# Fifteen of the eighteen adaLN vectors as running sums on the vector engine, in a two-layer hybrid DiT

## The chip, the cores and the metric

One core of a Trainium2 chip runs the whole program in one launch. The metric is the time on the device in microseconds; the number compared is the median of several runs. Engines: PE is the tensor engine (PEld its weight loads), DVE the vector engine, ACT the scalar engine, POOL GpSimd, SP the engine whose queue issues most DMAs.

## The reference: what is computed

Two layers over an image stream (512 tokens, x) and a context stream (256 tokens, c), each of 1024 features, all in float32. Each layer is a half FFN (hidden size 2816), a token mixing of three kinds (gated linear attention, sliding-window attention, RWKV7) with in- and out-projections, and a second half FFN. Nine vectors of 1024 per layer and stream, made from a conditioning vector, shift, scale and gate the three sub-layers:

```python
def adaln_params(cvec, w, b):
    m = jax.nn.silu(cvec) @ w + b              # [D] @ [D, 9 D]
    return m.reshape(cvec.shape[0], 1, N_MOD, D_MODEL)

def modulate(h, m, i):
    return h * (1.0 + m[:, :, 3 * i + 1]) + m[:, :, 3 * i]

def half_ffn(h, m, i, wg, wu, wd, g, b):
    u = modulate(h, m, i)
    return post_norm(h, 0.5 * m[:, :, 3 * i + 2] * swiglu(u, wg, wu, wd), g, b)

for l in range(DEPTH):                         # DEPTH = 2
    m_x = adaln_params(c, w_ada[l], b_ada[l])
    m_c = adaln_params(c_ctx[None], w_ada[l], b_ada[l])
    h_x = half_ffn(h_x, m_x, 0, ...)           # and h_c
    mix_x, mix_c = token_mixing(modulate(h_x, m_x, 1), modulate(h_c, m_c, 1), ...)
    h_x = post_norm(h_x, m_x[:, :, 5] * (mix_x @ w_out[l]), ...)
    h_x = half_ffn(h_x, m_x, 2, ...)           # h_c too, but not in the last layer
```

The 18 vectors (9 per layer, "vector 0" to "vector 8") take two products of a vector of 1024 with a matrix of 1024 x 9216 per layer. In layer 1 the context needs vectors 0 to 4 alone.

## The kernel before

Features lie on the partitions: a stream is 8 k-tiles of [128, tokens]. Every large product takes its operands as hi + lo parts, three PE products per pair (`product`); a block of weights, 4 k-tiles of 128 columns, is loaded by SP (`r_...`), copied by ACT to the hi part (`h_...`) and subtracted to the lo part (`l_...`) by DVE and POOL in turn (`load_split`). An FFN (`ffn`) makes 22 hidden tiles in six groups, two products each (`pg`, `pu`), and after each group eight down products (`py`), which DVE adds to the residue `r`. Names carry the stream, the layer and the FFN: `pgc00_4` is the gate product of hidden tile 4 of the context, layer 0, FFN 0.

The order of the program is `first(C)`, `mix(C, 0)`, `first(X)`, `mix(X, 0)`, `rest(C, 0)`, `mix(C, 1)`, `rest(X, 0)`, `mix(X, 1)`, `rest(X, 1)`, but a list scheduler with a model of the engines sets the order on each engine when the program is built, so that parts run beside each other: the context's mixing runs inside the image's FFN, and the image's mixing inside the context's later FFNs. On the chip each engine's queue runs in that order.

adaLN is cut into 72 chunks, 36 per layer, of 256 columns, four to a vector. A chunk (`ada_chunk`) is four loads of 256 KB (`wa`, eight buffers, later three) and eight PE products with 32 columns of the conditioning vectors (`sc`) as stationary and 256 columns of weights as moving operand. Four k-tiles go to four groups of 32 rows of a bank. After a vector's fourth chunk DVE copies the bank (`adr`), two products with the selector `c_sel` transpose and add the four groups, and DVE adds the bias (`ms`): `ada_tail`, run before the next vector. In the trace a float32 product is two rows. Chunks are placed by the program in two ways: `ada_some(between)`, behind each hidden tile of an FFN, takes `between` chunks from the list; `ada_need(l, i)` takes all up to vector i of layer l where it is used:

```python
        self.first(C, 0.5)
        self.first(X, 1)
        self.rest(C, 0, 1)
        self.rest(X, 0, 1)
```

Vectors 0 and 1 of layer 0 are needed before the first FFN product, as both modulate its input.

Of the kernel before, what the change touches and what calls it, by code (L numbers as in the profile page):

```python
# [9 lines left out]
F32 = mybir.dt.float32  # L10
# [4 lines left out]
ALU = mybir.AluOpType  # L15
# [22 lines left out]
# columns of the per-layer vector table  # L38
# [16 lines left out]
# tiles of the permuted input projection  # L55
T_RW = 0      # r0 r1 k0 k1 v0 v1 zw za zg
# [19 lines left out]
def _consts():  # L76
# [9 lines left out]
    # means of the halves of the partitions, in 16 rows each; back from such rows; a quarter of the rows  # L86
# [56 lines left out]
    # cosines, sines by row (8) and by column (64) of the grid, 1 where the feature turns by the other  # L143
# [20 lines left out]
class K:  # L164
# [3 lines left out]
    # ---------------------------------------------------------------- set-up  # L168
# [3 lines left out]
    def setup(self):  # L172
# [9 lines left out]
        cc = self.cp.tile([P, KT, 2], F32, name="cc")  # L182
# [3 lines left out]
        nc.scalar.activation(self.sc[:, :, 6:8], cc, AF.Silu)  # L186
        self.vec, self.ms, self.dv = [], [], []
# [55 lines left out]
    def weights(self, es, s, raw, n):  # L243
        """staging of the weights of an FFN"""
# [3 lines left out]
    def work_pool(self, es, s, name):  # L248
        """scratch of an FFN's stream"""
# [11 lines left out]
    # ---------------------------------------------------------------- adaLN  # L261
    def ada_chunk(self, l, ch):
        """256 columns of the modulation, a quarter of one vector, for both streams"""
        nc = self.nc
        i, cc = ch // 4, ch % 4
        if cc == 0:
            self.ada_tail()
            self.ada_ps = self.pln(f"ada{l}_{i}")
        ps = self.ada_ps
        for qt in range(4):  # L270
            w = self.wpool["f"][0].tile([P, 2, 256], F32, name=f"wa{l}_{ch}_{qt}", tag="wada", bufs=self.nada)
            nc.sync.dma_start(w, self.ins["ada"][l, ch, qt])
            for x in range(2):
                k = 2 * qt + x
                g = k % 4
                # row 32 g + 2 cc + stream: this quarter, the k-tiles of g
                nc.tensor.matmul(ps[32 * g:32 * g + 32, :256], self.sc[:, k, 6 - 2 * cc:38 - 2 * cc], w[:, x, :],  # L277
                                 start=cc == 0 and k < 4, stop=cc == 3 and k >= 4)
        if cc < 3:
            return  # L280
        r = self.wpool["f"][0].tile([P, 2, 256], F32, name=f"adr{l}_{i}", tag="wada", bufs=self.nada)[:, 0]
        nc.vector.tensor_copy(r, ps[:, :256])

        def tail():
# [3 lines left out]
            b = self.vec[l][:, V_BADA + 8 * i:V_BADA + 8 * i + 8].rearrange("p (a j) -> p a j", j=2)
            nc.vector.tensor_tensor(self.ms[l][i].rearrange("p (a j) s -> p a j s", j=2),
                                    ps[:, 256:272].rearrange("p (j a s) -> p a j s", j=2, s=2),  # L290
                                    b.unsqueeze(3).to_broadcast([P, 4, 2, 2]), ALU.add)
# [1444 lines left out]
```

## Time and profile before

| | us |
|---|---|
| median of 3 runs | 3524.41 |
| lowest, highest | 3515.36, 3530.89 |
| the profiled execution: span, first to last instruction | 3523.2 |
| PE busy in it | 3295.0 (94%) |
| DVE busy | 1824.8 (52%) |
| ACT busy | 1489.5 (42%) |
| POOL busy | 1513.6 (43%) |
| the 1152 rows of the adaLN products on PE | 147.5 |

For the profiled execution the page gives its span as its time; what lies around it is not shown apart. Busy times are unions over an engine's instructions; products overlap in the pipeline, so a row's length is not its cost. DVE's and POOL's rows hold their waits for each other. The mean granted clock of PE over the span is 0.96 of full speed.

### The profile page before, as it was taken

The numbers are of one execution on the slowest core, as the hardware profiler recorded it, in microseconds if no ns is written. First come the engines' busy times: TensorE is split into PE (matmuls) and PEld (weight loads), VectorE is DVE, ScalarE is ACT, GpSimd is POOL, SyncE is SP. The second block draws the span as 40 slices with busy tenths as digits, with TensorE's granted clock in tenths as the row PEclk, the third lists the DMA queues.
The fourth block names the chain that finished last, engine by engine and source line by source line (L and its number), as shares of the span: only waits on it lengthen the run. The fifth ranks groups of instructions, "written<-read, shape, count | busy, mean of one in ns | idle before, by whom it ended". The sixth has DMA issues, their size and how long they took to land. (4 is left out here: it accounts for less than half of the span.)

```text
span 3523.2 us, 63899 instructions
## 1 busy us (share of the span) xinstructions
PE 3295.0 (94%) x24774; PEld 2668.2 (76%) x24774; DVE 1824.8 (52%) x3198; ACT 1489.5 (42%) x2835; POOL 1513.6 (43%) x1375
## 2 busy tenths in 40 slices
PE   7999999999899999999989999899997997889997
PEld 4797667776677788789867888688885765678886
DVE  2545453445865556566767332542237666762224
ACT  2445333444553445456644433343335335643233
POOL 2554432434644455564454333533345343263335
PEclk8999999999999999999999999999998987999999
DMA  8765444344355543334242333223322210033332
GB/s 300 238 193 172 138 123 136 127 128 142 125 160 181 175 123 115 101 101 130 92 126 65 103 100 96 82 88 98 96 87 72 62 49 11 30 102 96 96 96 75
DMA packets 279135, 407.77 MB, mean 116 GB/s; under 512 B 76464, under 2 KB 101040, under 8 KB 278832
## 3 DMA queue, kind: packets, MB, share of 16 engines
q1 hardware_dynamic: 272064, 397.53, 36.2%
q10 hardware_dynamic: 6768, 6.16, 0.6%
q8 instruction: 195, 3.19, 0.4%
q14 instruction: 108, 0.88, 0.1%
HBM read 390.20 MB, written 13.39 MB: 115 GB/s over the span
## 5 line engine op out<-in xcount | busy, mean ns | idle before, releaser
L348 PE MATMUL pyx<-hhx,l_dx 128*128 128x512 f32 x704 | 277.7, 395 | 4.4 <-DVE l_dx L326 3.2
L348 PE MATMUL pyx<-hhx,h_dx 128*128 128x512 f32 x704 | 275.5, 393 | 0.3 <-ACT h_dx L323 0.3
L348 PE MATMUL pyx<-hlx,h_dx 128*128 128x512 f32 x704 | 275.5, 391 | 0.0
L437 DVE SCALAR_TENSOR_TENSOR rx<-pyx,gtx,rx 128x512 f32<-128x512 f32 x192 | 143.0, 748 | 239.2 <-PE pyx L348 239.1
L326 POOL TENSOR_TENSOR l_ux<-r_ux,h_ux 128x512 fp32r<-128x512 f32 x88 | 114.5, 1301 | 316.5 <-ACT h_ux L323 308.8
L323 ACT ACTIVATE h_dx<-r_dx 128x512 fp32r<-128x512 f32 (+1 forms) x192 | 113.5, 595 | 297.3 <-PE pyx L348 117.8
L323 ACT ACTIVATE h_ux<-r_ux 128x512 fp32r<-128x512 f32 x176 | 111.0, 631 | 280.0 <-PE pgx L348 137.7
L348 PE MATMUL pgx<-uhx,h_gx 128*128 128x512 f32 x528 | 209.2, 396 | 16.1 <-ACT uhx L543 16.1
L323 ACT ACTIVATE h_gx<-r_gx 128x512 fp32r<-128x512 f32 x176 | 111.0, 630 | 267.1 <-PE pyx L348 93.7
L348 PE MATMUL pgx<-ulx,h_gx 128*128 128x512 f32 x528 | 207.6, 393 | 5.9 <-DVE ulx L544 5.9
L326 POOL TENSOR_TENSOR l_dx<-r_dx,h_dx 128x512 fp32r<-128x512 f32 (+1 forms) x96 | 117.4, 1225 | 215.0 <-ACT h_dx L323 201.3
L326 POOL TENSOR_TENSOR l_gx<-r_gx,h_gx 128x512 fp32r<-128x512 f32 x88 | 120.0, 1363 | 204.4 <-ACT h_gx L323 196.0
L348 PE MATMUL pgx<-uhx,l_gx 128*128 128x512 f32 x528 | 207.4, 393 | 0.0
L348 PE MATMUL pux<-uhx,h_ux 128*128 128x512 f32 x528 | 207.1, 392 | 0.0
L348 PE MATMUL pux<-uhx,l_ux 128*128 128x512 f32 x528 | 206.5, 391 | 0.0
L348 PE MATMUL pux<-ulx,h_ux 128*128 128x512 f32 x528 | 206.4, 391 | 0.0
L354 POOL TENSOR_TENSOR hlx<-sgx,hhx 128x512 fp32r<-128x512 f32 x88 | 115.2, 1309 | 151.7 <-ACT hhx L353 151.4
L326 DVE TENSOR_TENSOR l_ux<-r_ux,h_ux 128x512 fp32r<-128x512 f32 x88 | 64.4, 731 | 205.9 <-ACT h_ux L323 205.3
L277 PE MATMUL ada<-wa,sc 128*32 128x256 f32 x1152 | 147.5, 405 | 19.7 <-DMA wa<-in_ada 14.2
L348 PE MATMUL pyc<-hhc,h_dc 128*128 128x256 f32 x528 | 154.9, 295 | 7.2 <-DVE rc L437 5.6
L348 PEld LDWEIGHTS pyx<-hhx,l_dx 128*128 128x128 f32 x704 | 132.6, 188 | 37.3 <-DVE l_dx L326 5.2
L348 PEld LDWEIGHTS pyx<-hhx,h_dx 128*128 128x128 f32 x704 | 132.6, 188 | 32.0 <-ACT h_dx L323 3.0
(800 smaller groups left out, 10153.3 us busy)
## 6 DMA issues: line engine op xcount, KB each, us to landing
wa<-in_ada SPq DMA_DIRECT2D x288, 256.0 KB, 3.8
r_gx<-in_wg SPq DMA_DIRECT2D x176, 256.0 KB, 2.7
r_ux<-in_wu SPq DMA_DIRECT2D x176, 256.0 KB, 2.7
r_gc<-in_wg SPq DMA_DIRECT2D x132, 256.0 KB, 3.0
r_uc<-in_wu SPq DMA_DIRECT2D x132, 256.0 KB, 3.0
r_dx<-in_wd SPq DMA_DIRECT2D x128, 256.0 KB, 2.7
r_dc<-in_wd SPq DMA_DIRECT2D x96, 256.0 KB, 3.0
r_ix<-in_win SPq DMA_DIRECT2D x84, 256.0 KB, 2.7
```

The source lines that it names most:

```text
L277: nc.tensor.matmul(ps[32 * g:32 * g + 32, :256], self.sc[:, k, 6 - 2 * cc:38 - 2 * cc], w[:, x, :], start=cc == 0 and k < 4, stop=cc == 3 ...
L323: nc.scalar.activation(hi[:, :n], raw[:, :n], AF.Copy)
L326: e.tensor_tensor(lo[:, :n], raw[:, :n], hi[:, :n].bitcast(F32), ALU.subtract)
L348: nc.tensor.matmul(ps[:, :N], wt[:, k, :], mv[kk][:, :N], start=kk == 0 and a == 0, stop=kk == n - 1 and a == 2)
L354: self.nc.gpsimd.tensor_tensor(lo, src, hi.bitcast(F32), ALU.subtract)
L437: nc.vector.scalar_tensor_tensor(r[j], py[:, :n], gt[:, j:j + 1], r[j], ALU.mult, ALU.add)
```

## The change

Vectors 0 to 2 of layer 0 stay on PE, in the same products, but a chunk is one load of 1 MB instead of four of 256 KB, and its tail follows at once. The other 15 vectors go in halves of 512 columns: for each of 8 k-tiles one load of 256 KB (`wa`, name tag `wadd`), and per stream one DVE instruction that multiplies the [128, 512] block by the stream's factor per partition and adds it to a running sum (`waa`, one buffer for both streams). Then PE sums over the partitions: per stream four products with 128 columns of the sum as stationary operand and a column of ones (`ones_c`) as moving one, and DVE adds the bias. Layer 1's vectors 5 to 8 are made for the image alone. The loads have buffers of their own (`apool`, four and later two). Units per hidden tile: 2.5 in `first(C)`, none in `first(X)`, 2 in `rest(C, 0)` and `rest(X, 0)`; a unit is one k-tile of a half, or a chunk of the first three vectors. `ada_flush` ends a half that is begun.

```diff
@@ setup
+        self.cc = self.sc[:, :, 6:8]
+        self.ones_c = self.cp.tile([P, 1], F32, name="ones_c")
+        nc.vector.memset(self.ones_c, 1.0)
@@ adaLN
-    def ada_chunk(self, l, ch):
+    def ada_chunk(self, l, i, cc):
...
-        for qt in range(4):
-            w = self.wpool["f"][0].tile([P, 2, 256], F32, name=f"wa{l}_{ch}_{qt}", tag="wada", bufs=self.nada)
-            nc.sync.dma_start(w, self.ins["ada"][l, ch, qt])
-            for x in range(2):
-                k = 2 * qt + x
-                g = k % 4
-                nc.tensor.matmul(ps[32 * g:32 * g + 32, :256], self.sc[:, k, 6 - 2 * cc:38 - 2 * cc], w[:, x, :],
-                                 start=cc == 0 and k < 4, stop=cc == 3 and k >= 4)
+        w = self.apool[0].tile([P, KT, 256], F32, name=f"wa{l}_{i}_{cc}", tag="wada", bufs=self.apool[1])
+        nc.sync.dma_start(w, self.ins["adap"][4 * i + cc])
+        for k in range(KT):
+            g = k % 4
+            nc.tensor.matmul(ps[32 * g:32 * g + 32, :256], self.sc[:, k, 6 - 2 * cc:38 - 2 * cc], w[:, k, :],
+                             start=cc == 0 and k < 4, stop=cc == 3 and k >= 4)
...
+    def ada_rows(self, l, i, h, k):
+        nc = self.nc
+        pool, bufs = self.apool
+        streams = (0,) if l == 1 and i >= 5 else (0, 1)
+        w = pool.tile([P, 512], F32, name=f"wa{l}_{i}_{h}_{k}", tag="wadd", bufs=bufs)
+        nc.sync.dma_start(w, self.ins["adad"][l, i, h, k])
+        if k == 0:
+            self.ada_acc = pool.tile([P, 2, 512], F32, name=f"waa{l}_{i}_{h}", tag="waa", bufs=1)
+        acc = self.ada_acc
+        for s in streams:
+            c = self.cc[:, k, s:s + 1]
+            if k == 0:
+                nc.vector.tensor_scalar(acc[:, s], w, c, None, ALU.mult)
+            else:
+                nc.vector.scalar_tensor_tensor(acc[:, s], w, c, acc[:, s], ALU.mult, ALU.add)
+        if k < KT - 1:
+            return
+        ps = self.pln(f"ada{l}_{i}_{h}")
+        n = len(streams)
+        for j in range(4):
+            for s in streams:
+                nc.tensor.matmul(ps[:, n * j + s:n * j + s + 1], acc[:, s, j * P:(j + 1) * P], self.ones_c,
                                  start=True, stop=True)
+        b = self.vec[l][:, V_BADA + 8 * i + 4 * h:V_BADA + 8 * i + 4 * h + 4]
+        nc.vector.tensor_tensor(self.ms[l][i][:, 4 * h:4 * h + 4, 0:n],
+                                ps[:, 0:4 * n].rearrange("p (j s) -> p j s", s=n),
+                                b.unsqueeze(2).to_broadcast([P, 4, n]), ALU.add)
+    def ada_unit(self, l, i, *a):
+        (self.ada_chunk if len(a) == 1 else self.ada_rows)(l, i, *a)
...
+    def ada_flush(self):
+        while self.pending and len(self.pending[0]) == 4 and self.pending[0][3]:
+            self.ada_unit(*self.pending.pop(0))
@@ first, rest
+            if s is C:
+                self.apool = self.pool(es, "adc0", "right"), 4
...
+            if s is C:
+                self.apool = self.pool(es, "adc1", "right"), 2
@@ run
-        self.pending = [(l, ch) for l in range(DEPTH) for ch in range(36)]
+        self.pending = [(0, i, cc) for i in range(3) for cc in range(4)]
+        self.pending += [(l, i, h, k) for l in range(DEPTH) for i in range(NMOD) if l or i > 2
+                         for h in range(2) for k in range(KT)]
         state = [{} for _ in range(DEPTH)]
-        self.first(C, 0.5)
+        self.first(C, 2.5)
         self.mix(C, 0, False, state[0])
-        self.nada = 3
-        self.first(X, 1)
+        self.first(X, 0)
         self.mix(X, 0, False, dict(state[0]))
-        self.rest(C, 0, 1)
+        self.rest(C, 0, 2)
         self.mix(C, 1, False, state[1])
         self.ces.close()
-        self.rest(X, 0, 1)
+        with ExitStack() as es:
+            self.apool = self.pool(es, "adx", "right"), 2
+            self.rest(X, 0, 2)
@@ layout
-    m["ada"] = f(a["w_ada"].reshape(DEPTH, 4, 2, P, 36, 256).transpose(0, 4, 1, 3, 2, 5))
+    m["adap"] = f(a["w_ada"][0, :, :3 * D].reshape(KT, P, 12, 256).transpose(2, 1, 0, 3))
+    m["adad"] = f(a["w_ada"].reshape(DEPTH, KT, P, NMOD, 2, 512).transpose(0, 3, 4, 1, 2, 5))
```

The scheduler's order changes with it. First DVE, in the context's first FFN, between the adds of hidden tiles 3 and 4 (`sgc00_3`, `sgc00_4`). Before:

```order
L416 TENSOR_TENSOR sgc00_3_721<-sgc00_3_721,puc00_3_684 128x256
L326 TENSOR_TENSOR l_uc00_4_0_785<-r_uc00_4_0_782,h_uc00_4_0_784 128x512
L282 COPY adr0_2_857<-ada0_2_549 128x256
L326 TENSOR_TENSOR l_dc00_0_0_0_868<-r_dc00_0_0_0_865,h_dc00_0_0_0_867 128x512
L289 TENSOR_TENSOR ms0_2_86<-ada0_2_549,vec0_82 128x16
L382 TENSOR_SCALAR gtc0_0_862<-ms0_2_86 128x8
L382 TENSOR_SCALAR gtx0_0_6855<-ms0_2_86 128x8
L416 TENSOR_TENSOR sgc00_4_818<-sgc00_4_818,puc00_4_781 128x256
```

and after the change, from the start of the second half of vector 3 (`waa0_3_1`):

```order
L304 TENSOR_SCALAR waa0_3_1_1083<-wa0_3_1_0_1081,sc_77 128x512 x2
L306 SCALAR_TENSOR_TENSOR waa0_3_1_1083<-wa0_3_1_1_1086,sc_77,waa0_3_1_1083 128x512 x2
L306 SCALAR_TENSOR_TENSOR waa0_3_1_1083<-wa0_3_1_2_1090,sc_77,waa0_3_1_1083 128x512
L351 TENSOR_TENSOR l_gc00_4_0_743<-r_gc00_4_0_740,h_gc00_4_0_742 128x512
L306 SCALAR_TENSOR_TENSOR waa0_3_1_1083<-wa0_3_1_2_1090,sc_77,waa0_3_1_1083 128x512
L306 SCALAR_TENSOR_TENSOR waa0_3_1_1083<-wa0_3_1_3_1175,sc_77,waa0_3_1_1083 128x512
L441 TENSOR_TENSOR sgc00_3_720<-sgc00_3_720,puc00_3_683 128x256
L306 SCALAR_TENSOR_TENSOR waa0_3_1_1083<-wa0_3_1_3_1175,sc_77,waa0_3_1_1083 128x512
L351 TENSOR_TENSOR l_uc00_4_0_780<-r_uc00_4_0_777,h_uc00_4_0_779 128x512
L306 SCALAR_TENSOR_TENSOR waa0_3_1_1083<-wa0_3_1_4_1179,sc_77,waa0_3_1_1083 128x512 x2
L351 TENSOR_TENSOR l_dc00_0_0_0_844<-r_dc00_0_0_0_841,h_dc00_0_0_0_843 128x512
```

There the splits (`l_gc`, `l_uc`, `l_dc`) and the hidden tile's add stand between the instructions of the running sum. Second PE, where vector 3 is made; before, in front of the second down product:

```order
L348 MATMUL pyc00_0_0_864<-hlc00_3_725,h_dc00_0_0_0_867 128x256
L348 MATMUL pyc00_0_0_864<-hhc00_3_724,l_dc00_0_0_0_868 128x256
L277 MATMUL ada0_3_1105<-wa0_12_0_1106,sc_77 32x256 x2
L277 MATMUL ada0_3_1105<-wa0_12_1_1110,sc_77 32x256 x2
L277 MATMUL ada0_3_1105<-wa0_12_2_1114,sc_77 32x256 x2
L348 MATMUL pyc00_0_1_884<-hhc00_0_464,h_dc00_0_1_0_887 128x256
L348 MATMUL pyc00_0_1_884<-hlc00_0_465,h_dc00_0_1_0_887 128x256
L348 MATMUL pyc00_0_1_884<-hhc00_0_464,l_dc00_0_1_0_888 128x256
```

and after the change, at the end of the up product of hidden tile 2, seven of the eight products that close the first half of vector 3:

```order
L373 MATMUL puc00_2_594<-uhc6_first_283,l_uc00_2_4_616 128x256
L373 MATMUL puc00_2_594<-uhc7_first_284,h_uc00_2_4_615 128x256
L373 MATMUL puc00_2_594<-ulc7_first_292,h_uc00_2_4_615 128x256
L373 MATMUL puc00_2_594<-uhc7_first_284,l_uc00_2_4_616 128x256
L313 MATMUL ada0_3_0_828<-ones_c_80,waa0_3_0_554 128x1 x7
L373 MATMUL pgc00_3_646<-uhc0_first_277,l_gc00_3_0_650 128x256
L373 MATMUL pgc00_3_646<-uhc1_first_278,h_gc00_3_0_649 128x256
L373 MATMUL pgc00_3_646<-ulc1_first_286,h_gc00_3_0_649 128x256
```

A half leaves eight products with a moving operand of one column in the place of sixteen with 256. Third PE at the context's first layer norm (`lnst`, `lnsq`, `lnm` and `lnb` are its small products). Before:

```order
L488 MATMUL lnsq_3447<-acc2_3259,c_ones_m_132 32x64 x4
L488 MATMUL lnsq_3447<-sq_3406,c_ones_m_132 32x64 x4
L493 MATMUL lnm_3474<-lnms_3468,c_eg_163 128x64 x4
L348 MATMUL pgx00_0_6305<-uhx0_first_6241,h_gx00_0_0_6308 128x512
L348 MATMUL pgx00_0_6305<-ulx0_first_6249,h_gx00_0_0_6308 128x512
L348 MATMUL pgx00_0_6305<-uhx0_first_6241,l_gx00_0_0_6309 128x512
L348 MATMUL pgx00_0_6305<-uhx1_first_6242,h_gx00_0_0_6308 128x512
L348 MATMUL pgx00_0_6305<-ulx1_first_6250,h_gx00_0_0_6308 128x512
```

and after the change:

```order
L513 MATMUL lnsq_3441<-acc2_3253,c_ones_m_134 32x64 x4
L513 MATMUL lnsq_3441<-sq_3400,c_ones_m_134 32x64 x4
L518 MATMUL lnm_3468<-lnms_3462,c_eg_165 128x64 x4
L518 MATMUL lnb_3474<-lnms_3462,c_eg_165 128x64 x4
L313 MATMUL ada0_6_0_3566<-ones_c_80,waa0_6_0_3224 128x1 x8
L373 MATMUL pic0_6_3613<-uhc0_0_1_3412,h_ic0_6_0_3430 128x256
L373 MATMUL pic0_6_3613<-ulc0_0_1_3420,h_ic0_6_0_3430 128x256
L373 MATMUL pic0_6_3613<-uhc0_0_1_3412,l_ic0_6_0_3431 128x256
```

The image's first gate product (`pgx00_0`) stood behind `lnm`; now the in-projection of the context (`pic0_6`), which needs the normalised context, comes next. On DVE, the image's modulation (`uf` and the scaling of `rx`, 16 instructions) moves likewise, from between the second down products to behind that layer norm.

## Rows read from the trace of the kernel before

**Rows 1.** Windows by stage: us busy and (instructions) per engine, granted clock, DMA, GB/s.
```profile
0.00:42.60 42.60, 23.81 (x136) 7.24 (x136) 5.68 (x34) 4.06 (x8) 1.45 (x5) 0.82 0.94 314
...
64.00:182.00 118.00, 110.93 (x896) 95.95 (x896) 55.19 (x91) 49.31 (x91) 60.96 (x49) 0.99 0.69 227
...
285.00:870.00 585.00, 572.21 (x4206) 425.30 (x4205) 274.43 (x542) 237.14 (x481) 217.50 (x227) 0.99 0.44 139
870.00:935.00 65.00, 48.96 (x318) 41.91 (x317) 60.41 (x67) 33.53 (x60) 48.13 (x42) 0.87 0.43 145
...
1335.00:1715.00 380.00, 363.70 (x3821) 327.41 (x3820) 244.17 (x463) 210.35 (x409) 201.72 (x174) 0.96 0.35 110
```

**Rows 2.** The same columns, two parts of 935 to 1335 us.
```profile
935.00:1050.00 115.00, 110.30 (x810) 84.80 (x809) 81.03 (x133) 62.38 (x121) 61.14 (x68) 1.00 0.48 146
1050.00:1335.00 285.00, 273.81 (x2812) 228.77 (x2810) 167.38 (x318) 118.20 (x248) 134.06 (x133) 0.98 0.54 160
```

**Rows 3.** Windows of the adaLN products alone; PE, PEld, DVE, then as above.
```profile
64.00:182.00 118.00, 18.98 (x172) 6.67 (x172) 1.79 (x6) 0.99 0.69 227
182.00:285.00 103.00, 7.05 (x68) 2.69 (x68) 0.60 (x2) 1.00 0.54 164
285.00:870.00 585.00, 58.84 (x476) 18.92 (x476) 4.12 (x14) 0.99 0.44 139
935.00:1050.00 115.00, 11.65 (x84) 3.48 (x84) 0.59 (x2) 1.00 0.48 146
1050.00:1335.00 285.00, 33.82 (x256) 9.98 (x256) 2.33 (x8) 0.98 0.54 160
```

**Rows 4.** Timeline of PE at 137 and 141 us; start, us, instruction, count.
```profile
137.16 1.07 PE L277 MATMUL ada<-wa,sc 128*32 128x256 f32 x16
138.16 0.39 PE L348 MATMUL pyc<-hhc,h_dc 128*128 128x256 f32 x1
...
141.13 0.51 PE L286 MATMUL ada<-c_sel,adr 128*128 128x8 f32 x4
141.50 0.36 PE L348 MATMUL pyc<-hhc,h_dc 128*128 128x256 f32 x1
```

**Rows 5.** Timeline of PE, end of the start.
```profile
40.32 1.02 PE L286 MATMUL ada<-c_sel,adr 128*128 128x8 f32 x4 [0.53 <-DVE adr L282]
...
42.71 0.58 PE L348 MATMUL pgc<-uhc_first,h_gc 128*128 128x256 f32 x1 [1.36 <-ACT uhc_first L353]
```

**Rows 6.** Timelines of DVE and POOL: one alone, two beside POOL, one alone.
```profile
149.92 0.53 DVE L388 TENSOR_SCALAR uf<-rx,Ax,Bx 128x512 f32<-128x512 f32 x1
...
2282.55 1.74 DVE L515 TENSOR_TENSOR rx<-rx,shift 128x512 f32<-128x512 f32 x1
...
2283.71 5.06 POOL L515 TENSOR_TENSOR rx<-rx,shift 128x512 f32<-128x512 f32 x3
...
2295.56 0.74 DVE L538 SCALAR_TENSOR_TENSOR ut<-rx,Ax,acc 128x512 f32<-128x512 f32 x1
```

**Rows 7.** Groups of DVE, whole span, then 64 to 182; count, us, ns.
```profile
L538 DVE SCALAR_TENSOR_TENSOR ut<-rx,Ax,acc 128x512 f32<-128x512 f32 x40 | 44.6, 1164 | 0.0
...
L548 DVE SCALAR_TENSOR_TENSOR rx<-rx,agx,acc 128x512 f32<-128x512 f32 x40 | 31.3, 849 | 0.0
...
L388 DVE TENSOR_SCALAR uf<-rx,Ax,Bx 128x512 f32<-128x512 f32 x8 | 9.1, 1143 | 0.0
...
L1604 DVE TENSOR_SCALAR rx<-rx 128x512 f32<-128x512 f32 x8 | 7.1, 882 | 0.1
```

**Rows 8.** Timeline of PE at the context's first layer norm.
```profile
289.11 0.50 PE L348 MATMUL pgx<-uhx_first,h_gx 128*128 128x512 f32 x1 [0.33 <-ACT h_gx L323]
...
298.89 0.28 PE L348 MATMUL pic<-uhc,h_ic 128*128 128x256 f32 x1
```

**Rows 9.** Window at the image's modulation, columns as in the first group.
```profile
141.50:167.00 25.50, 18.80 (x136) 17.87 (x136) 24.97 (x39) 11.71 (x22) 18.76 (x13) 0.93 0.49 159
```

**Rows 10.** Waits of the DMA queue of SP; us, times, longest.
```profile
SPq L272 <- PE ada L277: 134.9, 98, 6.4
```

More of the change, by code (lines that the diff above doesn't have):

```diff
@@ L181, in setup @@
         C.up = self.pool(self.ces, "upc", "right")
-        cc = self.cp.tile([P, KT, 2], F32, name="cc")
+        cc = self.cp.tile([P, KT, 2], F32, name="ccv")
         nc.scalar.dma_start(cc, self.ins["cc"])
@@ L212, in setup @@
         self.nsplit = 0
-        self.nada, self.tail, self.pre = 8, None, {}
+        self.pre = {}
         self.wnames = []
@@ L279, in ada_chunk @@
         if cc < 3:
             return
-        r = self.wpool["f"][0].tile([P, 2, 256], F32, name=f"adr{l}_{i}", tag="wada", bufs=self.nada)[:, 0]
+        r = self.apool[0].tile([P, 256], F32, name=f"adr{l}_{i}", tag="wadr", bufs=1)
         nc.vector.tensor_copy(r, ps[:, :256])
-        def tail():
-            for j in range(2):
-                nc.tensor.matmul(ps[:, 256 + 8 * j:264 + 8 * j], r[:, j * P:(j + 1) * P], self.c["sel"],
-                                 start=True, stop=True)
[L288 to L291, printed above, removed]
@@ L293, in ada_chunk @@
-        self.tail = tail
-    def ada_tail(self):
-        if self.tail is not None:
-            t, self.tail = self.tail, None
-            t()
+        for j in range(2):
+            nc.tensor.matmul(ps[:, 256 + 8 * j:264 + 8 * j], r[:, j * P:(j + 1) * P], self.c["sel"],
+                             start=True, stop=True)
+        b = self.vec[l][:, V_BADA + 8 * i:V_BADA + 8 * i + 8].rearrange("p (a j) -> p a j", j=2)
+        nc.vector.tensor_tensor(self.ms[l][i].rearrange("p (a j) s -> p a j s", j=2),
+                                ps[:, 256:272].rearrange("p (j a s) -> p a j s", j=2, s=2),
+                                b.unsqueeze(3).to_broadcast([P, 4, 2, 2]), ALU.add)
@@ L303, in ada_some @@
             self.credit -= 1
-            self.ada_chunk(*self.pending.pop(0))
+            self.ada_unit(*self.pending.pop(0))
+    def ada_flush(self):
+        while self.pending and len(self.pending[0]) == 4 and self.pending[0][3]:
+            self.ada_unit(*self.pending.pop(0))
     def ada_need(self, l, i):
-        while any(x[0] < l or (x[0] == l and x[1] // 4 <= i) for x in self.pending):
-            self.ada_chunk(*self.pending.pop(0))
-        while self.pending and self.pending[0][1] % 4:
-            self.ada_chunk(*self.pending.pop(0))
-        self.ada_tail()
+        while any(x[0] < l or (x[0] == l and x[1] <= i) for x in self.pending):
+            self.ada_unit(*self.pending.pop(0))
     def load_split(self, ap, k0, n, name, lane):
@@ L1611, in first @@
             self.ln_next(s, 0, 1, (0, 0), r, pool, self.spill[s.name, 0])
+            self.ada_flush()
     def rest(self, s, l, between):
@@ L1628, in rest @@
                 self.ln_next(s, l + 1, 1, (l + 1, 0), r, pool, self.spill[s.name, l + 1])
+            self.ada_flush()
     def run(self):
```

2 lines of the change are left out of this document (removed).

## Prediction

> **What bounds the kernel now.** I read the table of busy times by stage first: it says which engine fills a stage, and which comes near. In the first pass of the context's FFN (64 to 182 us), PE is busy for 110.9 of 118 us, DVE for 55.2 and POOL for 61.0. In the image's first FFN (285 to 870) it is PE 572 of 585 and DVE 274 [rows 1]. From 870 on, where the second FFN of the context runs beside the image's mixing, DVE rises to 60.4 of 65 us and 244 of 380 [rows 1], and to 81.0 of 115 [rows 2]. So PE is the bound almost everywhere before 1715 us, and DVE is nearest to it in 870 to 1050.
>
> What the products for adaLN take of PE is seen in the rows of their tile: 19.0, 7.1, 58.8, 11.7 and 33.8 us busy in five stretches [rows 3]. Busy time overlaps the product behind: a burst of 16 rows is busy 1.07 us, and the next product starts 1.00 us after its start [rows 4]. I take 0.92 of the busy time: 17.5, 6.5, 54.1, 10.7 and 31.1, together 120 us.
>
> **Prices.** A product of the old tail is two rows in the trace; four rows end in front of a product that starts 0.37 us after them [rows 4]. The first is hidden, the others are 0.112 us apart. A new tail of two streams is eight products, 16 rows: 0.03 + 15 x 0.113 = 1.72 us; one of one stream is 0.82. There are 22 and 8: 44 us. The moving operand is 1 column instead of 8; no row shows that, and as the time of 8 columns is not that of streaming them I take the same price. At the start of the program, with the granted clock down to 0.82 on the mean of the stretch [rows 1], the same four rows took 1.02 us [rows 5]; that is the upper bound, a half then 3.5 us. Vector 2 stays on PE: four bursts of 1.0 us, three before 64 us, where two chunks stand now.
>
> The new DVE instructions read two SBUF tensors of 128x512 (364 of them), or one (52). The same shape in layer norm takes 0.74 us alone, and a one-tensor instruction 0.53; next to POOL, a two-tensor one took 1.74 us, while three on POOL took 5.06 us [rows 6]. So one of the two engines waits for the other. Two lines of layer norm have the very form of the new instruction (two SBUF tensors, a vector of factors): 40 of one average 1.164 us, where POOL works all the time, 40 of the other 0.849 [rows 7]. POOL is half busy in the FFN, 61.0 of 118 us [rows 1], so I take the second, 0.85 us, and for the one-tensor ones 0.53 x 1.15 = 0.61. The bounds are 0.74 and 0.53, and 1.16 and 1.14, the last the mean of such instructions in the context's FFN [rows 7]. GPSIMD Engine Reference of the Trainium skill (Specifications) says that POOL's SBUF interfaces are shared with VectorE, with contention for instructions with two SBUF inputs. The trace agrees: 1.74 against 0.74 us [rows 6]. It speaks against the change; the slower rival below works it out.
>
> **The sum, by stretch.**
> - Up to 42.6 us: the first FFN product stands at 42.71 [rows 5]. Eight chunks of 1.05 MB, 1.05 of ctx and six blocks of weights, 11.0 MB, now stand ahead of the last one needed; at 314 GB/s [rows 1] they land after 35 us. From the last tail to that product it is 2.4 us (40.32 to 42.71 [rows 5]), with the burst and the copy ahead some 4. I take 39 for 43, -4; four buffers of 1 MB could cost one whole transfer (+3), or the queue could run at its later rate (-9).
> - 64 to 182: the order puts 88 new instructions here (78 and 10). Taken from DVE are the copies and the 16 instructions of the image's modulation, 9.1 + 7.1 us [rows 7], which move behind the context's layer norm. DVE: 55.2 - 17.1 + 78 x 0.85 + 10 x 0.61 = 111. PE: 110.9 - 17.5 + 5 x 1.72 + 1.4 = 103. Both are queues in order, so I take 115 for 118: -3 (103 to 140: -15 to +22). Behind each new instruction wait splits, which PE uses a few us later.
> - 182 to 285: -6.5 + 1.7 = -5.
> - The context's layer norm, about 289 us: now the first image products fill it, from 289.11 to the first in-projection at 298.89 [rows 8]. They stand behind the in-projection afterwards, as the image's u isn't made yet; some 8 us of PE come open. The modulation itself then holds PE up again. It did so before at 141.5 to 167 (18.8 of 25.5 us busy [rows 9]); with in-projections to do meanwhile I take 4 of those 6.7 us. +12 (0 to +19).
> - 285 to 870: -54.1 + 1.7 = -52. DVE has room for its few new rows, and PE is 98% busy; -48 (-52 to -40).
> - 870 to 1050: 68 new instructions (58 and 10) for DVE: 60.4 + 81.0 + 55 = 197 of 180 us. PE alone would fall by 10.7 - 6.9. DVE takes the bound over: +15 (-4 to +40).
> - 1050 to 1335: DVE 167 + 63 = 231 of 285, so PE stays the bound: -31.1 + 8.6 = -22; bursts give some back: -17 (-22 to 0).
> - 1335 to 1715: six tails, +10. DVE 244 + 72 = 316 of 380; I add 8 for waits: +18 (+10 to +35).
> - Later: eight tails of one stream, +6.
>
> Together -4 - 3 - 5 + 12 - 48 + 15 - 17 + 18 + 6 = -26 us. The profiled span, 3523.2, is 1.2 us below the median of 3524.4; from the median, **3498 us**. PE's own work falls by 74; what is lost is where DVE has no room. The DMA queue: SP waited 98 times, 134.9 us, for the buffers that PE freed [rows 10]; after the change it waits for DVE, with four buffers and later two, and the weights are queued behind. I put nothing on it, as weights are loaded four or more blocks ahead; without that cover, waits like those would pass to PE, and two dozen of their mean of 1.4 us lie inside the upper bounds.
>
> **The rivals.**
> - DVE's work is hidden everywhere: every price at its lower bound, and PE alone counts. -4 - 15 - 5 + 9 - 52 - 4 - 22 + 10 + 6 = -77: 3447. For it: DVE is at half in most stretches; against it: 141 of 180 us in 870 to 1050.
> - Slower: DVE and POOL take turns at the higher price, 1.16 and 1.14 us. 64 to 182 becomes 38 + 90 + 11 = 140 (+22), 870 to 1050 becomes 141 + 79 = 220 (+40), 1050 to 1335 255 of 285 (-12), 1335 to 1715 346 of 380 (+30). With the rest -4 - 5 + 12 - 48 + 6: +41, 3565. For it: the mean of 1.164 us [rows 7], POOL half busy in the same stretch [rows 1]. Against: the 40 at 0.849 [rows 7]. Between 0.85 (-26) and 1.16 (+41) the sum is zero at a mean of 0.98 us for the two-tensor instruction.
> - The change doesn't take the load off PE: the tails run at the lower clock, as PE has gaps around them. 22 x 3.5 + 8 x 1.75 = 91 instead of 44 us: -26 + 47 = +21, 3545. Against: from 64 us on the granted clock is 0.96 or more in all these stretches but one [rows 1, 2].
>
> **How the numbers follow.** I give the forecast 0.45, all hidden 0.22, the higher price 0.23, dear tails 0.10. The forecast's own range is 3480 to 3515. Half a per cent is 17.6 us, about what a measurement of this kernel tells from no change. Below 3507 lie two thirds of the forecast (0.30) and the first rival (0.22): 0.52. Slower than 3542: two thirds of the higher price (0.16) and half of the tails (0.05): 0.21. The rest, 0.27, is the same. The range, 3450 to 3560, leaves out about half of the first rival and the upper half of the second.
>
> **What the profile after would show.** Two-tensor adaLN instructions of 0.8 to 0.95 us; under 0.8, all is hidden; over 0.98, the kernel is slower. DVE over 90% busy with PE in gaps between the second and third down product of the context, and again from 870 to 1050. The image's first FFN shorter by about 48 us, from the first to the last product. A gap of PE of about 8 us behind the context's first layer norm. Tails of 1.7 us. I am wrong if the image's first FFN is not shorter (then PE was not its bound), or if waits of PE for the DMAs of weights come up in the place of those for DVE.

## The result, and the profile after

The changed kernel takes 3626.32 us in the median of 4 runs (3623.74 to 3630.84), the one before 3525.8 us in the runs beside it: a ratio of 1.029, interval 1.027 to 1.031. It is some 100 us slower, where 26 us less were forecast. The profiled execution takes 3625.21 us, its span is 3623.4 us. PE is busy for 3258.9 us of it, 36 less than before; DVE for 2166.0, 341 more.

The stages after, with the columns of [rows 1] (PE, PEld, DVE, ACT, POOL, then the granted clock, DMA share and GB/s):

```profile
0.00:42.60 42.60, 15.01 (x136) 6.21 (x136) 8.42 (x37) 4.75 (x8) 1.46 (x5) 0.71 0.96 350
64.00:182.00 118.00, 99.90 (x782) 95.70 (x775) 103.38 (x151) 41.13 (x75) 51.75 (x38) 0.96 0.68 210
182.00:285.00 103.00, 96.48 (x755) 95.80 (x753) 62.00 (x92) 46.35 (x86) 57.69 (x50) 0.93 0.59 181
285.00:870.00 585.00, 551.54 (x3945) 445.07 (x3946) 327.49 (x590) 256.78 (x521) 256.53 (x253) 0.96 0.32 98
870.00:935.00 65.00, 48.80 (x274) 44.04 (x273) 62.26 (x71) 31.52 (x55) 45.73 (x41) 0.84 0.50 161
935.00:1050.00 115.00, 94.78 (x631) 77.68 (x629) 97.04 (x159) 55.94 (x106) 54.66 (x56) 0.88 0.44 128
1050.00:1335.00 285.00, 254.97 (x2577) 234.28 (x2575) 228.21 (x372) 118.39 (x247) 144.84 (x130) 0.95 0.50 151
1335.00:1715.00 380.00, 342.05 (x3600) 303.96 (x3597) 282.02 (x476) 178.94 (x332) 206.19 (x168) 0.95 0.43 134
1715.00:1860.00 145.00, 107.32 (x875) 89.09 (x875) 95.68 (x238) 82.80 (x178) 38.97 (x50) 0.90 0.19 62
```

Against [rows 1, 2], PE is busy for less in every stage that both show, 95 of 115 us in the place of 110 and 255 of 285 in the place of 274, and DVE for more: 103 of 118 in the place of 55, 97 of 115 in that of 81, 228 of 285 in that of 167. In 1050 to 1335 no engine is full any more. The last row answers to no row ahead of the prediction; before, it was:

```profile
1715.00:1860.00 145.00, 117.12 (x947) 95.94 (x945) 106.05 (x190) 73.87 (x154) 72.12 (x75) 0.89 0.33 104
```

Where the time went is seen from the starts of products that both kernels have. Their names come from laying the program's order over the trace's rows; the prediction's column is the running sum of its terms.

| starts | before, us | after, us | shift | forecast |
|---|---|---|---|---|
| first FFN product | 42.7 | 46.6 | +3.9 | -4 |
| context FFN 1, third group of down products | 181.8 | 191.0 | +9.1 | -7 |
| context FFN 1, last down products | 273.9 | 286.6 | +12.7 | -12 |
| image FFN 1, first product | 289.1 | 317.3 | +28.2 | 0 |
| image FFN 1, last down products | 859.3 | 840.4 | -18.9 | -48 |
| context FFN 2, first product | 964.0 | 1002.5 | +38.5 | |
| context FFN 3, first product | 1352.1 | 1347.5 | -4.6 | -50 |
| context FFN 3, last down products | 1704.0 | 1725.7 | +21.8 | -32 |
| image FFN 2, first product | 1860.6 | 1942.8 | +82.2 | -32 |
| image FFN 2, last down products | 2253.6 | 2343.3 | +89.7 | -26 |
| image FFN 4, first product | 3133.3 | 3234.1 | +100.8 | -26 |

The forecast is some 127 us too low in all. 29 of them come up to 859 us, the rest behind it; the largest piece, 60 us, lies between the end of the context's third FFN and the start of the image's second (1726 to 1943 us after), where one tail and no sum stands.

One jump in the table is made up for later: the context's second FFN starts 38.5 us late. From the context's out-projection to it 135 us pass in the place of 79, with 48 sums (43.5 us) between and DVE busy for 121.5 of the 135. Its last down products come 12 us earlier than before all the same (1312.6 against 1324.6).

What is late between 1726 and 1943 us is the image's mixing. Its RWKV begins with the in-projection 6 (the first product named `pix`) and the part ends where in-projection 10 starts. Before:

```profile
894.08 0.51 PE L348 MATMUL pix<-uhx,h_ix 128*128 128x512 f32 x1 [0.63 <-ACT uhx L543]
...
1406.56 0.40 PE L348 MATMUL pix<-uhx,h_ix 128*128 128x512 f32 x1
```

and after:

```profile
876.33 0.49 PE L373 MATMUL pix<-uhx,h_ix 128*128 128x512 f32 x1 [0.64 <-ACT uhx L568]
...
1503.55 0.50 PE L373 MATMUL pix<-uhx,h_ix 128*128 128x512 f32 x1 [1.32 <-ACT glz L1119]
```

From the one to the other it is 512.5 us before and 627.2 after: in-projection 10 is 97 us late, though the stretch began 18 us earlier. The context's FFNs, which run beside it, have lost nothing when the third starts (-4.6 us), so they are finished when the mixing is not, and PE has gaps until it is: 107 of 145 us busy in 1715 to 1860 and 171 of the 217 us from 1725.7 to 1942.8; before, these gaps ended at 1860. The whole stretch, before and after:

```profile
894.10:1406.60 512.50, 479.48 (x4484) 399.93 (x4485) 335.70 (x587) 244.11 (x492) 261.40 (x263) 0.96 0.49 149
876.30:1503.60 627.30, 543.34 (x4844) 488.63 (x4844) 519.98 (x834) 279.23 (x549) 323.38 (x288) 0.92 0.49 149
```

DVE is busy in it for 336 us before and for 520 after, and 184 of these are the sums: its other work is the same. It stood idle for 177 us before and for 107 after. So 70 us of the sums went into time in which DVE had nothing to do; the other 114 are what the stretch is longer by.

One piece of that stretch on DVE shows how it becomes longer. A small triangular inverse runs there as a chain of steps (`MLx`, `TYx`), each waiting for the last; DVE's timeline before, from its first step to its last:

```profile
1021.32 0.28 DVE L761 TENSOR_SCALAR sgx<-sgx 32x256 f32<-32x256 f32 x1 [6.21 <-DMA sgx<-im1x]
...
1025.55 0.21 DVE L788 TENSOR_REDUCE TYx<-MLx 64x16 f32<-64x64 f32 x1
1025.69 0.67 DVE L326 TENSOR_TENSOR l_gc<-r_gc,h_gc 128x512 fp32r<-128x512 f32 x1
1026.29 0.21 DVE L783 TENSOR_TENSOR MLx<-sgx,TYx 64x64 f32<-64x64 f32 x1
...
1031.90 0.75 DVE L792 COPY sgx<-TYx 32x256 f32<-32x256 f32 x1
```

and after:

```profile
1025.47 0.28 DVE L786 TENSOR_SCALAR sgx<-sgx 32x256 f32<-32x256 f32 x1 [4.75 <-DMA sgx<-im1x]
...
1034.93 0.20 DVE L810 TENSOR_REDUCE TYx<-MLx 64x16 f32<-64x64 f32 x1
1035.06 0.67 DVE L351 TENSOR_TENSOR l_gc<-r_gc,h_gc 128x512 fp32r<-128x512 f32 x1
1035.66 0.73 DVE L306 SCALAR_TENSOR_TENSOR waa<-wa,sc,waa 128x512 f32<-128x512 f32 x1
1036.33 0.41 DVE L437 SCALAR_TENSOR_TENSOR sgc<-sgc,pgc 128x256 f32<-128x256 f32 x1
1036.66 1.44 DVE L306 SCALAR_TENSOR_TENSOR waa<-wa,sc,waa 128x512 f32<-128x512 f32 x1
1038.02 0.25 DVE L811 TENSOR_TENSOR MLx<-TYx 64x64 f32<-64x64 f32 x1
...
1058.15 1.33 DVE L817 COPY sgx<-TYx 32x256 f32<-32x256 f32 x1
```

Before, 11 us pass from the start of the first step to that of the last (1021.32 to 1031.90); after, 33 (1025.47 to 1058.15). Between the reduction at 1034.93 and the step at 1038.02 that uses it stand a split, two sums of 0.73 and 1.44 us and an add. In the trace DVE runs them one behind the other in the program's order, so a step of 0.25 us comes behind all of them. Not all of the 22 us are sums: in the 33 us stand 18 sums with 15 us, and 16 splits and adds of the context's FFN with 11 us, in the place of 4 with 2.6. The order was made anew, and it puts more of the FFN between the steps too.

The instructions of the sums, over the whole span (count | us, mean ns | idle before):

```profile
L306 DVE SCALAR_TENSOR_TENSOR waa<-wa,sc,waa 128x512 f32<-128x512 f32 x364 | 343.0, 971 | 45.1 <-DMA wa<-in_adad 44.6
...
L304 DVE TENSOR_SCALAR waa<-wa,sc 128x512 f32<-128x512 f32 x52 | 37.0, 743 | 7.1 <-DMA wa<-in_adad 7.1
```

Their mean is 0.971 us for the two-tensor ones and 0.743 for the others. And the start, on DVE, between the last vector's bias (`ms`) and the image of the context's input that PE needs (`uf`):

```profile
41.26 0.17 DVE L286 TENSOR_TENSOR ms<-ada,vec 128x16 f32<-128x16 f32 x1
41.35 1.40 DVE L306 SCALAR_TENSOR_TENSOR waa<-wa,sc,waa 128x512 f32<-128x512 f32 x2
42.67 0.17 DVE L393 TENSOR_SCALAR Ac<-ms 128x8 f32<-128x8 f32 x1
42.74 0.75 DVE L306 SCALAR_TENSOR_TENSOR waa<-wa,sc,waa 128x512 f32<-128x512 f32 x1
43.41 0.69 DVE L351 TENSOR_TENSOR l_ic<-r_ic,h_ic 128x512 fp32r<-128x512 f32 x1
44.01 1.75 DVE L306 SCALAR_TENSOR_TENSOR waa<-wa,sc,waa 128x512 f32<-128x512 f32 x1
45.68 0.72 DVE L413 TENSOR_SCALAR uf<-rc,Ac,Bc 128x256 f32<-128x256 f32 x2
```

PE's first FFN product comes behind it:

```profile
46.59 0.58 PE L373 MATMUL pgc<-uhc_first,h_gc 128*128 128x256 f32 x1 [5.88 <-ACT uhc_first L378]
```

From `ms` to `uf` four sums and a split stand, 4.4 us in the place of 0.4 before. Before, PE stood still for 1.36 us there [rows 5]; now for 5.88.

### The profile page after: what moved, and what is told of

The parts are those of the page before. It is cut to its first block, busy times and chain, and to the rows that moved or that the text cites. A ratio compares the mean times of both kernels' runs of the same rounds, so it can differ in the third digit from the quotient of the medians.

```text
span 3623.4 us, 63224 instructions
## 1 busy us (share of the span) xinstructions
PE 3258.9 (90%) x24170; PEld 2720.5 (75%) x24170; DVE 2166.0 (60%) x3615; ACT 1500.7 (41%) x2841; POOL 1576.7 (44%) x1375
## 5 line engine op out<-in xcount | busy, mean ns | idle before, releaser
L306 DVE SCALAR_TENSOR_TENSOR waa<-wa,sc,waa 128x512 f32<-128x512 f32 x364 | 343.0, 971 | 45.1 <-DMA wa<-in_adad 44.6
L373 PE MATMUL pyc<-hhc,l_dc 128*128 128x256 f32 x528 | 154.5, 294 | 9.6 <-DVE l_dc L351 9.4
L373 PE MATMUL pix<-uhx,h_ix 128*128 128x512 f32 x336 | 146.0, 435 | 18.3 <-ACT uhx L568 6.6
```

The costliest lines, as they stand in the source:

```text
L306: nc.vector.scalar_tensor_tensor(acc[:, s], w, c, acc[:, s], ALU.mult, ALU.add)
L373: nc.tensor.matmul(ps[:, :N], wt[:, k, :], mv[kk][:, :N], start=kk == 0 and a == 0, stop=kk == n - 1 and a == 2)
```

## The experiments

Three theories were held against each other. **Chain:** the sums stand in front of the dependent DVE steps of a mixing, and the mixing becomes longer by a share of their time. **PE:** the loss is the new tails, and the lower clock in gaps. **Loads:** the sums' loads, with few buffers, hold the weights up. Each kernel starts from the changed one. Ratios are to the kernel before, in runs on the same chip; its median there was 3519 to 3526 us, so microseconds taken between kernels of different sets are good to some 7. The scheduler orders every kernel anew, so each has another order on the engines as well.

**restc_pe: the sums beside the image's mixing are products again.**

```diff
+        for l in range(DEPTH):
+            for i in range(NMOD):
+                if l or i > 2:
+                    if (l == 0 and i > 5) or (l == 1 and i < 5):
+                        self.pending += [(l, i, cc) for cc in range(4)]
+                    else:
+                        self.pending += [(l, i, h, k) for h in range(2) for k in range(KT)]
...
-        self.rest(C, 0, 2)
+        self.rest(C, 0, (1, 1))
```

> The eight vectors that the context's second and third FFN make are products on PE again (32 chunks of four 256 KB loads, one per hidden tile); the other sums stay on DVE. Chain theory (the 200 or so sum instructions on DVE between 870 and 1400 us stand in front of the small dependent DVE steps of the image's RWKV and put its mixing 97 us late, of which 103 us show between 870 and 1860): the image's in-projection 10 is no longer late and the whole takes 3515 to 3545 us, though PE gets 32 x 1.0 us of products back. PE theory (the loss is the 16 tails there and the lower clock that gaps bring): only the tails' 27 us less 32 us of products, so 3620 to 3640. Load theory (256 KB loads with two buffers hold up the weights behind them): as many bytes in the same buffers, so no change, 3615 to 3635.

Measured: 3542.5 us, 1.0058 (1.0040 to 1.0075). The stretch from in-projection 6 to 10 takes 497.6 us, and in-projection 10 starts 49 us earlier than before:

```profile
859.50:1357.10 497.60, 445.42 (x4263) 354.27 (x4264) 294.25 (x525) 209.78 (x425) 213.12 (x222) 0.95 0.52 164
```

This is inside the chain theory's range; the PE and load theories are 70 us and more off. But the 49 us do not arrive: the image's second FFN starts at 1868.5 us, 7.9 later than before. Here the context's FFNs are late instead, the second starting at 1011.6 us (964.0 before) and the third reaching its last down products at 1745.2 (1704.0). From the context's out-projection to its second FFN it takes 79 us before, 78 to 91 in three kernels that make no vector there (combo_late, x00_rows2, x10_rows_b), 116 and 118 in two that make products there (restc_pe, x10_rows), and 134 to 140 in three with 48 sums (the change, c00_pe, x_late). So part of the loss behind 859 us may come from making vectors just there, on either engine, that were made earlier before; how much, no run tells.

**narrow: the sums cost DVE less, all loads and tails stay.** Part of the adaLN sums is left out: k-tiles 1 to 7 are added for 32 of 512 columns. The order changes with it: of DVE's 3616 instructions 2012 stand in the same place as in the change.

```diff
-                nc.vector.scalar_tensor_tensor(acc[:, s], w, c, acc[:, s], ALU.mult, ALU.add)
+                nc.vector.scalar_tensor_tensor(acc[:, s, :32], w[:, :32], c, acc[:, s, :32], ALU.mult, ALU.add)
```

> The sum instructions of k-tiles 1 to 7 work on 32 of the 512 columns (part of the adaLN sums is left out); loads, tails and their places in the program stay. Chain theory: some 260 us of DVE time are gone, the image's mixing is not late, 3450 to 3500 us. PE theory (tails, clock): the tails are all there, 3590 to 3630. Load theory: no change, 3610 to 3630.

Measured: 3535.8 us, 1.0043 (1.0029 to 1.0057): some 90 us less than the change, with every tail and load in the program, so the PE and load theories fall. Of these, 32 us are won up to the last down products of the context's first FFN, 40 up to those of the image's first, and another 47 between these and the image's second FFN. But the time is 36 us above the chain theory's range. The instructions didn't vanish; in the stretch they still take 78.6 us of DVE (the columns are PE, PEld and DVE of the tile `waa` alone):

```profile
836.00:1391.50 555.50, 25.97 (x192) 26.47 (x192) 78.55 (x182) 0.93 0.48 149
```

The stretch takes 555.5 us, 43 more than before. So although the image's first FFN ends 59 us earlier than before, in-projection 10 comes 15 us earlier only. DVE also waits for the sums' loads there for 32 us, where it is 11 in the change: the loads are not quite without a part.

**x00_rows: the sums moved beside the context's mixing, in the image's first FFN.**

```diff
-            if s is C:
-                self.apool = self.pool(es, "adc0", "right"), 4
+            self.apool = self.pool(es, "adc0" if s is C else "adx0", "right"), 4 if s is C else 2
...
-        self.first(X, 0)
+        self.first(X, 4)
...
-        self.rest(C, 0, 2)
+        self.rest(C, 0, (0, 2))
```

> Four units per hidden tile in the image's first FFN (176 of the sum instructions move there), none in the context's second FFN, two in its third. Room theory (DVE has room where PE is 95% busy: 327 of 585 us, plus 160 is 490): the image's first FFN stays as long as after the change, the image's mixing is on time, 3520 to 3550. Chain theory in its strong form (any sum instruction beside a mixing delays it, here the context's): the context's mixing ends some 100 us later than the image's FFN, 3590 to 3640.

Measured: 3739.0 us, 1.0613 (1.0591 to 1.0635), beyond both. Nearly none of these sums ran beside the FFN: from 840 to 1073 us 176 of them ran alone, one half after the other. The waits of that stretch (us, times, longest) show PE behind DVE at ten tails, and the image's layer norm standing for 183 us:

```profile
ACT shift L479 <- PE shift L478: 183.3, 1, 183.3
...
PE ada L313 <- DVE waa L306: 151.0, 10, 21.6
DVE waa L306 <- DMA wa<-in_adad: 40.5, 38, 2.0
```

The buffers were put on the side of SBUF on which the context's mixing lies. In the built program they have the place of its results (`mo_c`); POOL's last split of these ends at 849.9 us, and the first load of these sums is issued at 850.15. So they waited until that memory came free. The run says nothing on the theories.

**x00_rows2: the same, with the buffers on the image's side.** The other edits are those of x00_rows.

```diff
+            if s is X:
+                self.apool = self.pool(es, "adx0", s.side), 2
```

> As the run before with the rows in the image's first FFN, but their buffers lie on the image's side of SBUF: there the 11 halves waited for the memory of the context's mixing and ran alone, from 840 to 1073 us. Now the order spreads them over the second half of that FFN. Room theory: the image's FFN and the context's mixing end as after the change (840 and 867 us), the image's mixing later gets only the rows of the context's third FFN and is at most 30 us late, 3520 to 3560 us. Chain theory in its strong form: the context's mixing ends 60 to 100 us later than 867, 3580 to 3640.

Measured: 3595.9 us, 1.0208 (1.0187 to 1.0229), in the chain theory's range. Now 192 sum instructions, 165 us of DVE, lie between the context's in-projection 6 and its out-projection, and that stretch takes 617.6 us, 557.9 in the change and 586.0 before; it ends at 929 us, 62 later than after the change. The image's RWKV has 28 beside it and is nearly as long as before, 521.1 us (the tile `waa` alone):

```profile
939.30:1460.40 521.10, 5.80 (x32) 5.79 (x32) 25.77 (x28) 0.95 0.39 122
```

The lengthening went with the sums from one mixing to the other. DVE's room in that FFN was no help.

**x_late: a dose.** Of layer 1's vectors 0 to 4 the image's sums are made later, from a second load.

```diff
-        streams = (0,) if l == 1 and i >= 5 else (0, 1)
+        streams = (0,) if (l == 1 and i >= 5) or self.late else (1,) if l == 1 else (0, 1)
...
+        self.late = True
+        self.pending = [(1, i, h, k) for i in range(NMOD) for h in range(2) for k in range(KT)]
...
-            self.rest(X, 0, 2)
+            self.rest(X, 0, 3.5)
```

> A dose: of layer 1's vectors 0 to 4 the context's sums stay in place, the image's are made from a second load of the weights in the image's later FFNs, where PE is busy all the time and DVE a third of it. So 80 of the 256 sum instructions leave the context's second and third FFN. Chain theory: the 115 us by which the image's RWKV stretch is longer (627 against 512 us from in-projection 6 to 10) fall in proportion, to 65 to 90, and the whole to 3575 to 3605, with 8 us of new one-stream tails in the image's FFNs in it. Load and PE theories: tails and loads become more, 3625 to 3650.

Measured: 3595.4 us, 1.0205 (1.0188 to 1.0222), with more tails and more loads than the change. The stretch holds 136 sum instructions, 125.6 us, where the change has 202, 184.0 us. The tile `waa` alone, in x_late:

```profile
876.10:1469.60 593.50, 19.24 (x144) 19.89 (x144) 125.64 (x136) 0.92 0.49 153
```

and in the change:

```profile
876.30:1503.60 627.30, 28.83 (x208) 29.15 (x208) 183.96 (x202) 0.92 0.49 149
```

It takes 593.5 us, 81 more than before; 65 to 90 were expected.

**bufs4: four buffers for those loads.**

```diff
-                self.apool = self.pool(es, "adc1", "right"), 2
+                self.apool = self.pool(es, "adc1", "right"), 4
```

> Four buffers for the loads of the sums in the context's later FFNs in the place of two. DVE stood 11 us in that stretch waiting for such loads, with the steps of the mixing queued behind. Load theory: the sums' loads and the weights behind them on SP's queue come in time, 3560 to 3600. Chain theory: the sums themselves take the time, 3612 to 3630.

Measured: 3725.1 us, 1.0575 (1.0554 to 1.0597). Neither range holds it, and the load theory was not tested: the first sum's load was issued at 1230.5 us, when the image's in-projection 10 stood at 1230.8, and the context's second FFN began at 1335. In the built program the larger pool reaches into memory of the image's RWKV (its tiles `Zx` and `TYx`; `Zx` is last read at 1217 us), so the first load had to come behind that. By that it measured something else, the image's RWKV with neither FFN nor sums beside it (most of the context's out-projection is in it, and the granted clock is 0.73):

```profile
867.40:1230.80 363.40, 217.74 (x2161) 173.86 (x2161) 176.41 (x310) 106.90 (x217) 104.54 (x129) 0.73 0.15 43
```

So it takes 363 us there. Beside the context's FFN it takes 512 (before), beside FFN and sums 627 (the change).

**c00_pe: vectors 3 to 5 of layer 0 as products.**

```diff
+                    if l == 0 and i < 6:
+                        self.pending += [(l, i, cc) for cc in range(4)]
...
-        self.first(C, 2.5)
+        self.first(C, 0.75)
```

> Vectors 3 to 5 of layer 0 are products on PE again inside the context's first FFN (12 chunks), the rest as in the change. If the 18 us that the context's first FFN and the start lose against before come from the sums there: that FFN ends 10 to 15 us earlier, and the whole takes 3605 to 3620. If they come from the larger loads of the first three vectors, which stay: 3620 to 3640.

Measured: 3607.7 us, 1.0246 (1.0225 to 1.0266), 18.6 less than the change (some 15 by the ratios). The first FFN product starts at 40.40 us with the 1 MB loads still there, and PE's gap is that of before:

```profile
40.40 0.58 PE L380 MATMUL pgc<-uhc_first,h_gc 128*128 128x256 f32 x1 [1.37 <-ACT uhc_first L385]
```

The context's first FFN reaches its last down products at 268.0 us, 18.6 before the change's and 5.9 before those of the kernel before. So up to there the sums cost 18.6 us more than the products, 6.2 of them at the start and 12.4 in the FFN, where no mixing runs. The start without sums is 2.3 us earlier than before, with the larger loads and the tail that follows at once.

**combo_late, x10_rows, x10_rows_b: tries at a faster version.** combo_late puts together c00_pe, the sums of layer 0's vectors 6 to 8 and of the context's in layer 1 in the image's first FFN, and the image's of layer 1 in its later FFNs.

```diff
-        self.first(C, 2.5)
+        self.first(C, 0.75)
...
-        self.first(X, 0)
+        self.first(X, 6)
...
-        self.rest(C, 0, 2)
+        self.rest(C, 0, 0)
```

> An attempt at a faster version: vectors 3 to 5 of layer 0 as products in the context's first FFN, vectors 6 to 8 and the context's 0 to 4 of layer 1 as sums in the image's first FFN (six units per tile), nothing in the context's later FFNs, all the image's sums of layer 1 in its later FFNs. If sums beside the context's mixing cost nothing: 3440 to 3490. If they delay it as they delay the image's: the mixing ends 50 to 100 us later, 3520 to 3580.

Measured: 3580.8 us, 1.0167 (1.0140 to 1.0195), at the upper end of the slower range. The context's mixing, with 160 sums (136 us) beside it, takes 644.1 us, 86 more than in the change; the image's RWKV, with no sum beside it, 497.0.

x10_rows keeps sums only for the image's last four vectors, in its third FFN, where no mixing runs; x10_rows_b has 0.4 chunks per tile in the image's first FFN.

```diff
+                    if l == 0 or i < 5:
+                        self.pending += [(l, i, cc) for cc in range(4)]
...
-        self.rest(C, 0, 2)
+        self.rest(C, 0, (0.6, 0.6))
...
-            self.rest(X, 0, 2)
+            self.rest(X, 0, (0, 3))
```

> A version for speed by the chain theory: sums on DVE only where no mixing runs beside (the image's vectors 5 to 8 of layer 1, three units per hidden tile in the image's third FFN, 64 sum instructions, 8 one-stream tails); all else products: layer 0 up to vector 5 in the context's first FFN, none in the image's first FFN, 32 chunks in the context's later FFNs. Chain theory: the image's third FFN is 6 to 8 us longer for its tails, no stage has a late mixing, the start is 2 us earlier, and PE has 8 chunks of 1 us less net: 3495 to 3520, at or a little below before. If sums cost time wherever they stand: that FFN is longer by 64 x 0.66 = 42 us, 3540 to 3560.

> The same with 0.4 chunks per hidden tile (some 9) in the image's first FFN, taken from the context's second. If PE sets the time of the image's first FFN and the mixing that of the stretch behind it, 9 chunks cost 9 us there and give back less: 3500 to 3530, slower than its twin by 3 to 9 us. If the burst of chunks ahead of the context's second FFN holds the chain: faster than its twin.

Measured: 3525.2 us, 1.0012 (1.0000 to 1.0025), and 3529.9 us, 1.0019 (1.0007 to 1.0030). Neither is faster than before (x10_rows missed its range by 5 us), and the two are not told apart. In x10_rows the image's RWKV takes 485.1 us and the image's second FFN starts 26 us earlier than before. It then gives 14 us back: the context's second mixing began 24 us later than before and that FFN 26 us earlier, so more of the mixing runs inside it, 2352 PE rows in 407 us (first row) where 2167 took 393 before. The third FFN, with the sums and eight tails, takes 358.3 us, 8.6 more than before:

```profile
1834.00:2241.00 407.00, 401.32 (x2352) 328.12 (x2353) 174.38 (x294) 151.09 (x275) 145.96 (x120) 0.98 0.31 97
2274.00:2633.00 359.00, 353.38 (x1562) 292.30 (x1563) 159.17 (x228) 115.55 (x192) 133.60 (x97) 0.98 0.38 124
```

6 to 8 were expected; 64 sums would be 42 us if they cost their time. Here, with no mixing beside them and DVE busy for 159 of 359 us, they are hidden.

The image's RWKV over all kernels but bufs4 (sum instructions and their DVE time are those of the stretch):

| kernel | in-projection 6 to 10, us | sum instructions | DVE, us |
|---|---|---|---|
| x10_rows | 485.1 | 0 | 0 |
| combo_late | 497.0 | 0 | 0 |
| restc_pe | 497.6 | 4 | 3 |
| x10_rows_b | 511.4 | 16 | 15 |
| x00_rows | 511.7 | 32 | 26 |
| before | 512.5 | 0 | 0 |
| x00_rows2 | 521.1 | 28 | 26 |
| narrow | 555.5 | 182 | 79 |
| x_late | 593.5 | 136 | 126 |
| c00_pe | 617.3 | 194 | 183 |
| after | 627.3 | 202 | 184 |

The length follows the sums' DVE time, and not their number: narrow has more of them than x_late, and is 38 us shorter. Against before, a microsecond of that time makes the stretch longer by 0.57 (c00_pe) to 0.64 us (x_late) in the kernels with more than 100 us of it, and by 0.55 in narrow. The seven kernels with 0 to 26 us of sums lie between 485 and 521 us and say little on this price. What the new order does by itself is in all these numbers: no kernel has the order of another with the sums taken out.

## Why the prediction was wrong

**The bound.** The step that failed is the first: "PE is the bound almost everywhere before 1715 us", read from busy shares. From 870 us on the image's mixing is a chain of dependent steps; its RWKV takes 363 us in bufs4, with neither FFN nor sums beside it, 512 before, and 627 with the sums, and PE has to wait for the mixing's end. PE was 96% busy before in three of those four windows [rows 1, 2] because the order fills it with the context's FFNs, and these are finished first; taking products from PE there does not make the mixing end sooner. By the same step the sum said for 1050 to 1335 that DVE would have 231 of 285 us to do and "PE stays the bound". DVE has 228.2 of 285: the load was right, and the conclusion was not. In 935 to 1050, with DVE at 84%, the step at 1038.02 already stands behind sums. The terms +15, -17 and +18 came to +16; from the image's last down products to the context's last it was 41 us (-18.9 to +21.8).

**"Later: eight tails of one stream, +6."** From the first product of the image's FFN 2 to the last down products of its FFN 3, 9.7 us were lost, near that. But the 60 us between 1704 and 1861 fell into no term: the sum followed the context's stages as if the image's mixing would be done with them.

**The price of a sum** was forecast at 0.85 us (0.74 to 1.16), measured 0.971, and 0.61 (0.53 to 1.14), measured 0.743. By the prediction's own line a mean of 0.98 makes the sum zero (0.97 on a straight line between its two points); the kernel is 100 us slower at 0.97. The higher-price rival had the right sign, but its mechanism makes some 26 us of the miss at this price, not 127. That POOL raises the price held: in the change the 202 two-tensor sums whose time overlaps an instruction of POOL took 1.156 us in the mean, the 162 others 0.741, and none of these over 0.753. GPSIMD Engine Reference of the Trainium skill (Specifications) has the two engines share SBUF interfaces, with contention where a DVE instruction reads two SBUF inputs; the two means agree with it.

**Up to 285 us** the forecast was -12, measured +12.7. At the start four sums and a split stand between `ms`, `Ac` and `uf`, and the prediction put nothing on them (39 us forecast, 40.40 in c00_pe without them, 46.6 with). The stretch behind it was forecast at -8 and came out at +8.8, inside the bounds of its larger term, -15 to +22.

**What held.** The context's layer norm and the move of the image's modulation: +12 forecast, +15.5 measured. The image's first FFN: -48 forecast, -47.1 measured (+28.2 to -18.9); there the products did come off PE's path. The tails at the higher clock: a one-stream one takes 0.81 us from its first row to the next product (0.82 forecast):

```profile
2471.65 0.95 PE L313 MATMUL ada<-ones_c,waa 128*128 128x1 f32 x8
2472.46 0.48 PE L373 MATMUL pgx<-uhx,h_gx 128*128 128x512 f32 x1
```

A two-stream one took 1.71 us at 264.5 us (1.72 forecast). All together are 55.5 us with 4 us of waits in it, where 44 were forecast; three took 3.43 us. The rival of dear tails needed 91 us, and narrow has every tail.

**Open.** How much of the loss is the sums' own time on DVE, and how much the new order and the place where the vectors are made, is not told apart: no run kept the order. 9 us were lost in the image's second mixing, between 2760 and 3177 us, where no sum runs; in x00_rows2 that stretch is 8 us shorter than before. No run was made on it. Whether more buffers for the loads help was not found out.

## What to carry to other kernels

A list of busy shares shows which engine has work, not which work is waited for: an engine that the order keeps 95% full with work that nothing waits for yet may have slack, and one at 50% may lie on a chain. Before work is moved to an engine with room, look for a serial chain that passes through that engine in the same stretch, and price each instruction moved there as a part (here some 0.6) of its length on the chain, not as nothing until the engine is full. Sums hid in the image's third FFN (x10_rows, DVE at 44%); they cost 12.4 us more than products in the context's first, with DVE at 103 of 118 us, and they cost wherever much of them ran beside a mixing.

## What the runs showed of the hardware

In narrow, a DVE instruction of 128x32 in the place of 128x512 took 0.436 us in the mean of 158 in one stretch, against 0.967 for 176 of the full width in the change: a sixteenth of the columns, not quite half of the time. Over the whole of narrow, the 212 that overlap no instruction of POOL took 0.244 us in the mean, the 152 others 0.696. In the changed kernel's own start the mean granted clock was 0.71, lower than before [rows 1], with PE busy for 15 of 42.6 us. Three two-stream tails, at 305.8, 878.8 and 1344.1 us, took 3.43 us, twice the 1.71 of others: 0.214 us for a row, where 0.107 is usual. The granted clock was 0.50 (1.2 GHz) while they ran, and 1.00 (2.4 GHz) during the one at 264.5.
